# Side work beside the products of a hybrid attention and gating layer, laid out anew

## The chip, the cores and the metric

The kernel runs on one core of a Trainium2 chip. Its time is the device time of one execution in microseconds (us). Before the change the median of three runs is 1669.73 us (1668.16 to 1673.44). The engines are named as the profile names them: PE is TensorE (its weight loads are PEld), DVE is VectorE, ACT is ScalarE, POOL is GpSimd and SP is SyncE, which issues most of the DMAs; POOL issues the others.

## The reference, cut to what matters

One layer of a decoder trunk for 512 tokens of width 2048, in float32:

```python
shift, scale, gate = split(silu(c) @ w_ada + b_ada, 3)
h = rmsnorm(x, attn_norm_g) * (1 + scale) + shift
q_lat, kv_lat, k_rope, z_mla, u, v, z_sgu, g_mla, g_sgu = split(h @ w_in)
q  = rmsnorm(q_lat, q_norm_g) @ w_uq        # 16 heads, 128 + 64 rotary
kv = rmsnorm(kv_lat, kv_norm_g) @ w_ukv     # 16 heads, 128 + 128
y_mla = causal_attention(q, kv, rotary(k_rope)) * silu(z_mla)
y_sgu = u * (tril(w_spatial) @ rmsnorm(v) + b_spatial) * silu(z_sgu)   # 16 groups, chunks of 128
x = x + gate * ((sigmoid(g_mla) * y_mla + sigmoid(g_sgu) * y_sgu) @ w_out)
return rmsnorm(x, final_norm_g)
```

The widths are: q_lat 768, kv_lat 512, k_rope 64, and 2048 for each of z_mla, u, v, z_sgu, g_mla, g_sgu.

## The kernel before, in words

**Products.** Every float32 operand is split into a high part, which ACT makes by a cast, and a low part, which DVE makes by a subtraction (`hilo`, L139 to L141, and `split_to`, L92 to L112). Each product is then three matmuls, high by high, low by high and high by low (`mm3`, L134 to L137, and L1159 to L1161).

**The stages**, in order of the program:

1. The latents (q_lat, kv_lat) and one head's columns from x, weights w1 and w2. What the additive `shift` contributes to them (its "share") isn't in these products and is added much later.
2. v and k_rope, weights wv, in forty granules, each a weight tile with 24 matmuls. Beside it DVE makes the last third of the conditioning (`ada_dot`, 128x2048), scales the thirteen latent tiles by the norm of x and stores them in HBM (`lat_scale`), and forms sums and differences of blocks of h (`make_s12`, `make_s4`) for the next stage.
3. The pairs: the columns of z, g, u, s (z_sgu) and t (g_sgu) of two heads are taken as a pair, and their products with two halves of the tokens are done in seven products of half size instead of eight, after Strassen's scheme. There are 38 pairs. One of the seven products of a pair is a *step* (the code says slot) of 24 matmuls of 128x256. The steps are numbered -4 to 265; the steps -4 to -1 hold a plain product of one head's columns, and step 0 is the first of the pairs. Product p of pair k stands in a list `order`; products of one pair add up in one PSUM bank, and between two of them the bank's value is read out ("evacuated") by ACT (p = 1, 2, 4, 6) or DVE (p = 3, 5, 7).
4. Attention, 16 heads, then the output product and the last norm.

**What sets the order around the change.** The engines take their instructions strictly in the order in which the kernel's code issues them; there is no scheduler. In the pairs' stage an event is put on a step with `on(step, phase, f)`. Each step runs its events by phase: FIRST, EVAC, GATE, SPLIT, BACK ahead of the step's matmuls, MISC and LOAD behind them. The weight tile of step s is split in step s - 2 (SPLIT). Side work is put in BACK; loads and stores in LOAD. In the second stage the work of a granule hangs in `early[granule]`.

**The side work beside the pairs**, before the change:

- *Third differences* (`make_s3`, L742 to L746): for each of eight blocks of h, hh + hl, left half minus right half, split again; in BACK of steps -2 to 2. The results are the operands of product 3.
- *Spatial gating* (`sgu_*`): scale, split, 16 small matmuls, output, once for each of the 16 groups.
- *Share* (`share_load`, `share`, L840 to L860): w1 and w2 are loaded a second time, and DVE adds shift times each row block into four accumulators. One load of 512 KB (w1) or 320 KB (w2) into one buffer `raw3` every three steps, from step 44 on, and two DVE instructions three steps later; `shift_bias` sums them up from step 143 on.
- *Latents* (`lat_load`, `lat_sq`, `lat_rstd`, `lat_norm`, `last_gates`, L880 to L940): each latent tile (256 KB) comes back from HBM into one of two buffers (`rx`, `sinT`), first for the sum of squares, then, after the reciprocal root, to be normalised and stored again. A tile every two steps, loaded three steps ahead, steps 149 to 201.
- *Rotary tables* (`rope_part`, L946 to L1032): sine and cosine of position times frequency, in four quarters of 128 columns, two functions of a chain in each of 22 steps, 209 to 230. The last two functions of a quarter end in a Sin on ACT.
- *The rotary key*, steps 232 to 238, and the first splits for the attention at the end.

Of the kernel before, what the change touches and what calls it, by code (L numbers as in the profile page):

```python
# [20 lines left out]
P = 128  # L21
# [94 lines left out]
def trunk_layer(ctx, tc, xT, xn, c, vecs, pos, wada, w1, w2, wv, wv3, wv4, wh, wh15, wq, wqr, wk, wvv, wo, wsT, bsp, gfin, out,  # L116
# [340 lines left out]
    def split_sum(name, j, src):  # L457
        h, l = sums[name + "h"][:, j], sums[name + "l"][:, j]
        hilo(h, l, src)
# [10 lines left out]
    def make_s4(j):  # L470
        a, b = (nt(tb.p, [P, S], F32, f"t{i}") for i in range(2))
        tt(a[:, left], sums["s2h"][:, j].bitcast(F32), sums["s2l"][:, j].bitcast(F32), ALU.add)
        tt(b[:, left], hh[j + 8].bitcast(F32)[:, left], hl[j + 8].bitcast(F32)[:, left], ALU.add)
        tt(a[:, left], a[:, left], b[:, left], ALU.add)
        split_sum("s4", j, a[:, left])

    def lat_scale(i):
        tt(lat[i], lat[i], rx, ALU.mult)
        DMA.dma_start(lat_d[i], lat[i])

    for i in range(13):
        early.setdefault(8 + i, []).append(lambda i=i: lat_scale(i))
    for j in range(8):
        early.setdefault(11 + 2 * j + j // 2, []).append(lambda j=j: make_s12(j))
        early.setdefault(32 + j, []).append(lambda j=j: make_s4(j))
    for cg, w in enumerate(VW):
        psv = [bank()[:, :w] for _ in range(4)]
        for i in range(8):
# [17 lines left out]
            for f in early.pop(g, ()):  # L506
                f()
        if cg == 0:
# [6 lines left out]
        def evac_v(n, cg, ps):  # L515
            m = VW[cg] // P
            w, c0 = m * P, sum(VW[:cg])
            junk = nt(tb.p, [P, S], F32, "sig", bufs=2)
# [3 lines left out]
            DMA.dma_start(v_d[n][:, c0:c0 + w], t[:, :w])  # L522
            if cg == 4:
                DMA.dma_start(kr_d[n], t[:, w:VW[cg]])
# [313 lines left out]
    share_raw = [None]  # L838

    def share_load(k):  # L840
        share_raw[0] = t = nt(mis.p, [P, GW], F32, "raw3")
        if k < KC:
            DMA.dma_start(t, w1[k])
        else:
            DMA.dma_start(t[:, :640], w2[k - KC])

    def share(k):

        raw, j = share_raw[0], k % KC
        if k == 0:  # L850
            acc.extend([slot("rx"), slot("sinT")])
        if k == KC:
            acc.extend([slot("cosT"), acc2])
        for a, lo_, w in ((0, 0, S), (1, S, S)) if k < KC else ((2, 0, S), (3, S, P)):
            o, i_ = acc[a][:, :w], raw[:, lo_:lo_ + w]
            if j == 0:
                ts(o, i_, shift[:, 0:1], None, ALU.mult)
            else:
                stt(o, i_, shift[:, j:j + 1], o, ALU.mult, ALU.add)
# [21 lines left out]
    def lat_load(i, n):  # L881
        lat_in[i] = slot(("rx", "sinT")[n % 2])
        DMA.dma_start(lat_in[i], lat_d[i])

    def lat_sq(i):
        t = lat_in.pop(i)
        if i in (0, 6):
            ss[0] = slot("cosT")
# [6 lines left out]
    def lat_rstd(n):  # L895
        pl = bank()
        PE.matmul(pl, ones.bitcast(F32), ss[0], start=True, stop=True)
        rstd_from(ss[0], pl, n)

    def lat_norm(i):  # L900
        t = lat_in.pop(i)
        stt(t, t, bias[:, i:i + 1], ss[0], ALU.add, ALU.mult)
        on(done[0], LOAD, lambda: DMA.dma_start(latn_d[i], t))

    def last_gates(i):
# [9 lines left out]
        if i == 10:  # L915
            ss["g"] = slot("cosT")
# [4 lines left out]
        def to_u():  # L921
            DMA.dma_start(out_d["g"][1][7], ss["g"])
            ss["u"] = slot("cosT")
# [8 lines left out]
    s_, n = s_bias + 6, 0  # L932
    for f, a in todo:
        if f is lat_rstd:
            on(s_, MISC, f, a)
            s_ += 1
# [9 lines left out]
    def rope_part(half):  # L946
        w = S // 4
# [13 lines left out]
        def new(k):  # L961
            n = "cdes".find(k)
            t[k] = tables["ba".index(k)][:, cl] if n < 0 else rt[0][:, n * w:(n + 1) * w]
# [36 lines left out]
        def s9():  # L1000
# [3 lines left out]
            ACT.activation(tables[1][:, cl], t["d"], AF.Sin, scale=vec[:, C_SGN:C_SGN + 1])  # L1004

        def s10():
            ts(t["s"], t["s"], 0.25, None, ALU.add)
            rnd(new("e"), t["s"], m23)
            tt(new("d"), t["s"], t["e"], ALU.subtract)
            ts(t["d"], t["d"], lim, -lim, ALU.min, ALU.max)  # L1010
            ACT.activation(tables[0][:, cl], t["d"], AF.Sin, scale=2.0 * math.pi)

        rope.extend([s0, s1, s2, lambda: frac("c", c1_, True), lambda: frac("c", c2_),
                     lambda: frac("b", d1 / 65536.0), lambda: frac("b", d2 / 65536.0), s7, s8, s9, s10])

    for part in range(4):
# [3 lines left out]
    def rope_begin():  # L1020
        rt.append(slot("rx"))
        tables.extend([slot("cosT"), slot("sinT")])
        DMA.dma_start(tables[0].bitcast(I32), bcast(pos, S))

    s_ += 2
    on(s_, LOAD, rope_begin)
    for i in range(0, len(rope), 2):
        on(s_ + 4 + i // 2, BACK, lambda i=i: [f() for f in rope[i:i + 2]])
    s_ += 6 + len(rope) // 2
# [3 lines left out]
    def key_load():  # L1033
        krn = nt(mis.p, [P, GW], F32, "raw3")[:, :S].rearrange("p (n a b) -> p n a b", n=NB, a=2)
# [28 lines left out]
    on(s_, LOAD, key_load)  # L1063
    on(s_ + 4, MISC, key_turn)
# [489 lines left out]
```

## Time and profile before

| what | value |
|---|---|
| median of three runs | 1669.73 us |
| the profiled execution's own time | 1674.57 us |
| its span, first to last instruction | 1672.8 us |
| mean granted TensorE clock | 0.986 |
| PE busy | 1614.9 us (97%) |
| DVE, ACT, POOL busy | 1203.1 us (72%), 767.0 us (46%), 103.7 us (6%) |
| read from and written to HBM | 303.36 MB, 23.99 MB |

The first stage takes up to 195 us of the span, the second up to 342, the plain product and the pairs up to 1196, attention up to 1500 and the output product the rest. Times of rows are counted from the span's start. A busy PE isn't a PE at its peak: matmuls overlap, and half of a full clock looks as busy as the whole, so the profile's column of the granted clock (PEclk) has to be read with it. In the list of waits a row tells which instruction waited, for which, for how long in all, how often and how long at most. In a timeline a bracket at the end is the idle time of the engine just before that instruction, and what ended it.

### The profile page before, as it was taken

What the parts mean: (1) busy time and instruction counts of PE and PEld (TensorE: products, weight loads), DVE (VectorE), ACT (ScalarE), POOL (GpSimd) and SP (SyncE); (2) the same over time, 40 slices, a digit from 0 to 9 for tenths busy, and PEclk for the clock granted to TensorE, in tenths of its full rate; (3) what the DMA queues carried; (4) which work ended last, traced back from release to release, by engine and by line L of the source; (5) the groups of instructions that cost most, each with busy time, mean ns of one, the idle gap of its engine ahead of it and who ended that gap; (6) DMA issues with size and microseconds to landing.
All of it is one profiled execution on the core that took longest, in us unless ns stands there. A gap on an engine that the chain in (4) does not pass through costs nothing.

```text
span 1672.8 us, 27059 instructions
## 1 busy us (share of the span) xinstructions
PE 1614.9 (97%) x10760; PEld 1503.1 (90%) x10760; DVE 1203.1 (72%) x1840; ACT 767.0 (46%) x1272; POOL 103.7 (6%) x127
## 2 busy tenths in 40 slices
PE   9999999969999999999999898899999999999997
PEld 7888889969999999999999898799898888888887
DVE  8988677766667777777677678776778778874453
ACT  4343333445445444454554545454555555542332
POOL 0000000001111111111111011102000000000000
PEclk9999999989999999999999999999999999999999
DMA  9987588447789998988788886578523232326432
GB/s 378 347 294 289 194 288 296 149 129 201 209 206 253 250 254 223 254 246 228 203 223 232 236 239 177 122 194 170 177 85 102 85 101 80 98 76 252 126 101 101
DMA packets 116864, 329.13 MB, mean 197 GB/s; under 512 B 13545, under 2 KB 31489, under 8 KB 109953
## 3 DMA queue, kind: packets, MB, share of 16 engines
q1 hardware_dynamic: 99008, 269.72, 46.0%
q0 software_dynamic: 17728, 57.68, 19.9%
q8 instruction: 84, 1.38, 0.3%
q14 instruction: 44, 0.35, 0.1%
HBM read 303.36 MB, written 23.99 MB: 196 GB/s over the span
## 4 chain that ended last, share of the span: by engine, by line
PE 79%; DVE 9%; DMA 6%; ACT 3%; issue 2%; SPq 0%; DVEq 0%; ACTq 0%
PE ps L136 14%; PE ps L137 14%; PE ps L135 14%; PE ps L1159 11%; PE ps L1161 11%; PE ps L1160 11%; DMA rx<-lat_d 2%; DMA latn_d<-rx 1%; DVE lat L123 1%; DVE w2l L123 1%; PE ps L1321 1%; DVE w0l L123 1%; DVE rx L123 1%; DVE w1l L123 1%; PE ps L1284 1%
## 5 line engine op out<-in xcount | busy, mean ns | idle before, releaser
L1159 PE MATMUL ps<-hh,w2h 128*128 128x256 f32 x400 | 115.8, 289 | 8.1 <-DVE lat L123 5.6
L1159 PE MATMUL ps<-hh,w0h 128*128 128x256 f32 x416 | 118.9, 286 | 3.5 <-DVE lat L123 3.5
L1161 PE MATMUL ps<-hh,w0l 128*128 128x256 f32 x416 | 118.3, 284 | 1.0 <-DVE w0l L123 1.0
L1160 PE MATMUL ps<-hl,w0h 128*128 128x256 f32 x416 | 118.4, 285 | 0.0
L106 DVE TENSOR_TENSOR w1l<-wraw,w1h 128x1024 fp32r<-128x1024 f32 (+3 forms) x74 | 73.1, 988 | 62.4 <-ACT w1h L105 61.0
L106 DVE TENSOR_TENSOR w0l<-wraw,w0h 128x1024 fp32r<-128x1024 f32 (+3 forms) x74 | 78.9, 1066 | 53.2 <-ACT w0h L105 52.5
L1161 PE MATMUL ps<-hh,w2l 128*128 128x256 f32 x400 | 115.1, 288 | 1.8 <-DVE w2l L123 1.8
L1160 PE MATMUL ps<-hl,w2h 128*128 128x256 f32 x400 | 114.8, 287 | 0.0
L1159 PE MATMUL ps<-hh,w1h 128*128 128x256 f32 x400 | 113.9, 285 | 0.0
L1161 PE MATMUL ps<-hh,w1l 128*128 128x256 f32 x400 | 113.4, 284 | 0.1
L1160 PE MATMUL ps<-hl,w1h 128*128 128x256 f32 x400 | 113.3, 283 | 0.0
L105 ACT CAST w0h<-wraw 128x1024 fp32r<-128x1024 f32 (+3 forms) x74 | 68.9, 931 | 94.0 <-PE ps L137 47.1
L105 ACT CAST w1h<-wraw 128x1024 fp32r<-128x1024 f32 (+3 forms) x74 | 63.8, 862 | 99.3 <-PE ps L137 43.3
L126 DVE SCALAR_TENSOR_TENSOR wada<-wada,cact 128x2048 f32<-128x2048 f32 x47 | 107.1, 2281 | 0.0
L123 DVE TENSOR_TENSOR w2l<-raw,w2h 128x1024 fp32r<-128x1024 f32 x56 | 68.4, 1222 | 37.2 <-ACT w2h L616 37.1
L136 PE MATMUL ps<-w0l,hh 128*128 128x256 f32 (+3 forms) x288 | 93.3, 324 | 1.9 <-DVE w0l L106 1.9
L135 PE MATMUL ps<-w0h,hh 128*128 128x256 f32 (+3 forms) x288 | 93.6, 325 | 0.9 <-ACT w0h L105 0.9
L137 PE MATMUL ps<-w0h,hl 128*128 128x256 f32 (+3 forms) x288 | 93.1, 323 | 0.0
L137 PE MATMUL ps<-hh,w1l 128*128 128x512 f32 x226 | 88.9, 394 | 2.0 <-DVE w1l L106 2.0
L135 PE MATMUL ps<-hh,w1h 128*128 128x512 f32 x226 | 90.4, 400 | 0.2 <-ACT hh L378 0.2
L136 PE MATMUL ps<-hl,w1h 128*128 128x512 f32 x226 | 88.9, 393 | 0.8 <-DVE hl L126 0.8
L596 POOL DMA_DIRECT2D wraw<-in_wh x66 | 58.5, 941 | 462.1 <-DVE w0l L123 203.6
(351 smaller groups left out, 5475.6 us busy)
## 6 DMA issues: line engine op xcount, KB each, us to landing
raw<-in_wh SPq DMA_DIRECT2D x105, 512.0 KB, 7.1
wada<-in_wada SPq DMA_DIRECT2D x47, 1024.0 KB, 7.2
wraw<-in_wh POOLq DMA_DIRECT2D x66, 512.0 KB, 7.1
wraw<-in_wh SPq DMA_DIRECT2D x45, 512.0 KB, 7.6
raw<-in_wh POOLq DMA_DIRECT2D x42, 512.0 KB, 7.1
wraw<-in_wo SPq DMA_DIRECT2D x32, 512.0 KB, 3.7
wraw<-in_w SPq DMA_DIRECT2D x16, 512.0 KB, 8.5
wraw<-in_wv SPq DMA_DIRECT2D x16, 512.0 KB, 4.8
```

What stands on the lines that cost most here:

```text
L105: self.nc.scalar.copy(hi[:, :n], raw[:, :n])
L106: self.nc.vector.tensor_tensor(out=lo[:, :n], in0=raw[:, :n], in1=hi[:, :n].bitcast(F32), op=ALU.subtract)
L123: DVE.tensor_tensor(out=out, in0=in0, in1=in1, op=op)
L126: DVE.scalar_tensor_tensor(out=out, in0=in0, scalar=scalar, in1=in1, op0=op0, op1=op1, **kw)
L135: PE.matmul(ps, ah, bh, start=start, stop=False)
L136: PE.matmul(ps, ah, bl, start=False, stop=False)
L137: PE.matmul(ps, al, bh, start=False, stop=stop)
L596: q_.dma_start(t, wh[h, n, q // 10 - 1], **eng)
L1159: PE.matmul(ps, wH[:, sl], xh, start=st, stop=False, skip_group_check=True)
L1160: PE.matmul(ps, wH[:, sl], xl, start=False, stop=False, skip_group_check=True)
L1161: PE.matmul(ps, wL[:, sl], xh, start=False, stop=sp, skip_group_check=True)
L1284: PE.matmul(ps, q2[:, q], krh[:, :n], start=False, stop=False)
```

## The change

Eight edits, none of which adds or removes a matmul:

1. **Third differences.** `make_s12`, `make_s4` and `make_s3` become one `make_sums` in the second stage. DVE forms all four results there; the first two are split one granule later, the third (kept in float32 in freed latent tiles) only in BACK of steps -2 to 1, two a step, and the fourth in granules 32 to 39.
2. **Stores of the second stage.** Stores of v, k_rope and the latents are put in a list and issued a granule later. The latents are scaled in another order, so that tiles come free in the order in which the sums need them. The squares in `evac_v` no longer share the two buffers of the stored copies.
3. **Share.** 52 loads of 256 KB in place of 32 of 512 or 320 KB, two buffers `half0` and `half1`, one load every two steps, four steps ahead, one DVE instruction of 512 columns each (the last four: four of 128 columns).
4. **Latents.** They use `half0` and `half1`; loads stand four steps ahead; a normalised tile comes every three steps and not every two, and is stored in MISC of the next step. `ss` moves from `cosT` to `rx`.
5. **Reciprocal.** The 128x512 reciprocal is cut into four of 128x128, one in each of four steps.
6. **Rotary tables.** Two halves of 256 columns instead of four quarters, one function a step, in steps 166 to 177 and 201 to 212 instead of 209 to 230; both Sin stand in a function of their own at the end of each half. The latents now run over steps 154 to 221, the share over 42 to 149.
7. **Rotary key.** Its steps are unchanged (232 to 238).
8. **First splits of the attention.** One step earlier.

```diff
-    def make_s12(j):
-        a, b = (nt(tb.p, [P, S], F32, f"t{i}") for i in range(2))
+    def make_sums(j):
+        a, b = (nt(tb.p, [P, S], F32, f"t{i}") for i in range(2))
         tt(a, hh[j].bitcast(F32), hl[j].bitcast(F32), ALU.add)
-        tt(b[:, right], hh[j + 8].bitcast(F32)[:, right], hl[j + 8].bitcast(F32)[:, right], ALU.add)
+        tt(b, hh[j + 8].bitcast(F32), hl[j + 8].bitcast(F32), ALU.add)
+        s3f[j], s4f[j] = half_of(S3_AT, j), half_of(S4_AT, j)
+        tt(s3f[j], a[:, left], a[:, right], ALU.subtract)
         tt(b[:, right], a[:, right], b[:, right], ALU.subtract)
-        split_sum("s1", j, b[:, right])
-        tt(b[:, left], b[:, right], a[:, left], ALU.subtract)
-        split_sum("s2", j, b[:, left])
...
+        tt(a[:, left], b[:, right], a[:, left], ALU.subtract)
+        tt(s4f[j], a[:, left], b[:, left], ALU.add)
+        return lambda: (split_sum("s1", j, b[:, right]), split_sum("s2", j, a[:, left]))
...
+    def stores():
+        for dst, src in leaving:
+            DMA.dma_start(dst, src)
+        leaving[:], made[:] = made[:], []
...
-    def make_s3(j):
-        a = slot(("rx", "lat12")[j % 2])
-        tt(a, hh[j].bitcast(F32), hl[j].bitcast(F32), ALU.add)
-        tt(a[:, left], a[:, left], a[:, right], ALU.subtract)
-        hilo(hh[j][:, right], hl[j][:, right], a[:, left])
-
     for j in range(8):
-        on(-2 + j * 2 // 3, BACK, make_s3, j)
+        on(-2 + j // 2, BACK, lambda j=j: hilo(hh[j][:, right], hl[j][:, right], s3f[j]))
...
-    s_share = base[6] + 4
-    for k in range(2 * KC):
-        on(s_share + 3 * k, LOAD, share_load, k)
-        on(s_share + 3 * k + 3, BACK, share, k)
-    s_bias = s_share + 6 * KC + 3
+    s_share = base[6] + 2
+    for i in range(len(shares)):
+        on(s_share + 2 * i, LOAD, share_load, i)
+        on(s_share + 2 * i + 4, BACK, share, i)
+    s_bias = s_share + 2 * len(shares) + 4
...
     def lat_rstd(n):
...
-        rstd_from(ss[0], pl, n)
+        ACT.activation(ss[0], pl, AF.Sqrt, bias=eps, scale=1.0 / n)
+        r = ss[0]
+        for q in range(4):
+            on(done[0] + 1 + q, BACK, lambda o=r[:, q * P:(q + 1) * P]: DVE.reciprocal(out=o, in_=o))
...
     def lat_norm(i):
         t = lat_in.pop(i)
         stt(t, t, bias[:, i:i + 1], ss[0], ALU.add, ALU.mult)
-        on(done[0], LOAD, lambda: DMA.dma_start(latn_d[i], t))
+        on(done[0] + 1, MISC, lambda: DMA.dma_start(latn_d[i], t))
...
-            on(s_ - 3, LOAD, lat_load, a, n)
+            on(s_ - 4, LOAD, lat_load, a, n)
...
-        s_ += 2
+        s_ += 3 if f is lat_norm else 2
...
+    on(base[22] + 9, LOAD, rope_begin)
+    for part in range(2):
+        s_ = base[22 + 5 * part] + 14
+        on(s_, FIRST, rope_places)
+        for i in range(12):
+            on(s_ + i, BACK, rope[12 * part + i])
...
-    on(n_slots - 1, SPLIT, lambda: ws.split_to(gr[0]))
+    on(n_slots - 2, SPLIT, lambda: ws.split_to(gr[0]))
+    on(n_slots - 1, MISC, lambda: ws.split_to(gq[0]))
```

**DVE at the opening of the pairs.** Before, its rows between the weight splits of steps 2 and 3 (`w1l`, `w0l`) hold two whole third differences: a sum of 512 columns, a difference of 256 and the low part, twice.

```order
L123 TENSOR_TENSOR lat_334_3159<-hh_158_1272,hl_160_1276 128x512
L123 TENSOR_TENSOR lat_334_3159<-lat_334_3159 128x256
L123 TENSOR_TENSOR hl_160_1276<-lat_334_3159,hh_158_1272 128x256
L123 TENSOR_TENSOR rx_3164<-hh_165_1352,hl_167_1356 128x512
L123 TENSOR_TENSOR rx_3164<-rx_3164 128x256
L123 TENSOR_TENSOR hl_167_1356<-rx_3164,hh_165_1352 128x256
L123 TENSOR_TENSOR lat_338_3197<-lat_330_3151,lat_331_3153 128x512
L123 TENSOR_TENSOR w0l_3200<-raw_311_3033,w0h_3199 128x1024
```

Now the rows there are the low parts alone (`lat_260` is a kept third difference), and the next step's rows follow.

```order
L123 TENSOR_TENSOR hl_167_1356<-lat_260_2373,hh_165_1352 128x256
L123 TENSOR_TENSOR hl_168_1358<-lat_260_2373,hh_166_1354 128x256
L123 TENSOR_TENSOR lat_325_3168<-lat_319_3128,lat_320_3130 128x512
L123 TENSOR_TENSOR w0l_3171<-raw_303_3017,w0h_3170 128x1024
L123 TENSOR_TENSOR hl_175_1416<-lat_282_2583,hh_173_1412 128x256
L123 TENSOR_TENSOR hl_176_1418<-lat_282_2583,hh_174_1414 128x256
L123 TENSOR_TENSOR raw_300_3011<-raw_300_3011,raw_302_3015 128x1024
```

The sums and differences have gone to the second stage; ACT's casts of the high parts stay where they were, two a step.

**SP in the latents' norms.** Before, the store of a normalised tile (`latn_d`) stands right behind the load of the tile after next, and a load into its buffer one weight load later.

```order
L883 DMA rx_9448<-lat_d_110 128x512
L903 DMA latn_d_122<-sinT_9380 128x512
L596 DMA raw_1128_9511<-in_wh 128x1024
L883 DMA sinT_9513<-lat_d_111 128x512
L903 DMA latn_d_123<-rx_9448 128x512
```

Now the store (`latn_d_120` from buffer `half_1129`) stands in the following step, and the next load into the same buffer (`half_1154`) behind one weight load; the loads for the spatial gating (`wsr`, `bsr`, `lat` from `v_d`) stand behind that load.

```order
L928 DMA latn_d_120<-half_1129_9507 128x512
L616 DMA raw_1153_9714<-in_wh 128x1024
L905 DMA half_1154_9716<-lat_d_109 128x512
L771 DMA wsr_9748<-in_wsT 128x256
L773 DMA bsr_9750<-in_bsp 128x256
L778 DMA lat_1159_9752<-v_d 128x4x128
L928 DMA latn_d_121<-half_1141_9612 128x512
```

What moved is the distance: a tile of the norms comes every third step, with the same order of store and load in the queue.

**DVE in the rotary tables.** Before, a step's rows are two functions of a quarter (128 columns), here with the gates' rows and the weight split `w1l` of the step after.

```order
L130 TENSOR_SCALAR rx_10530<-cosT_10531 128x128
L132 TENSOR_SCALAR rx_10530<-rx_10530 128x128
L123 TENSOR_TENSOR rx_10530<-rx_10530 128x128 x2
L132 TENSOR_SCALAR rx_10530<-rx_10530 128x128
L123 TENSOR_TENSOR rx_10530<-rx_10530 128x128
L126 SCALAR_TENSOR_TENSOR sinT_10532<-rx_10530,sinT_10532 128x128
L123 TENSOR_TENSOR lat_1238_10330<-lat_1238_10330,lat_1283_10744 128x512
L123 TENSOR_TENSOR lat_1238_10330<-lat_1251_10439,lat_1238_10330 128x512
L123 TENSOR_TENSOR w1l_10787<-wraw_1268_10596,w1h_10786 128x1024
```

Now they are one function of a half (256 columns), and every other step a latent's sum of squares stands ahead of it (`rx`, last row but four).

```order
L130 TENSOR_SCALAR lat_1083_9100<-cosT_8939 128x256
L132 TENSOR_SCALAR lat_1084_9101<-lat_1083_9100 128x256
L123 TENSOR_TENSOR lat_1083_9100<-lat_1083_9100,lat_1084_9101 128x256
L123 TENSOR_TENSOR lat_1084_9101<-lat_1084_9101,lat_1083_9100 128x256
L123 TENSOR_TENSOR lat_1091_9143<-ps_1109_9297,lat_1091_9143 128x256
L123 TENSOR_TENSOR wraw_1082_9096<-wraw_1082_9096,wraw_1089_9139 128x1024
L123 TENSOR_TENSOR w0l_9326<-wraw_1082_9096,w0h_9325 128x1024
L123 TENSOR_TENSOR rx_8952<-rx_8952,lat_1112_9329 128x512
L130 TENSOR_SCALAR lat_1083_9100<-cosT_8939 128x256
L132 TENSOR_SCALAR lat_1084_9101<-lat_1083_9100 128x256
L123 TENSOR_TENSOR lat_1083_9100<-lat_1083_9100,lat_1084_9101 128x256
L123 TENSOR_TENSOR lat_1084_9101<-lat_1084_9101,lat_1083_9100 128x256
```

The tables have moved from steps that hold no other side work but the gating to steps that hold the latents' work too.

More of the change, by code (lines that the diff above doesn't have):

```diff
@@ L477, in lat_scale, with store @@
+        tt(s4f[j], a[:, left], b[:, left], ALU.add)
+        return lambda: (split_sum("s1", j, b[:, right]), split_sum("s2", j, a[:, left]))
+    made, leaving = [], []
+    def store(dst, src):
+        made.append((dst, src))
+    def stores():
+        for dst, src in leaving:
+            DMA.dma_start(dst, src)
+        leaving[:], made[:] = made[:], []
     def lat_scale(i):
         tt(lat[i], lat[i], rx, ALU.mult)
-        DMA.dma_start(lat_d[i], lat[i])
-    for i in range(13):
-        early.setdefault(8 + i, []).append(lambda i=i: lat_scale(i))
+        store(lat_d[i], lat[i])
@@ L837, in trunk_layer, with half_raw, share_load, share @@
     acc = []
[L838 to L843, printed above, removed]
-        else:
[L845 to L856, printed above, removed]
+    share_raw = {}
+    def half_raw(i):
+        return nt(mis.p, [P, S], F32, f"half{i % 2}")
+    shares = [(q, (k,), w1[k][:, q * S:(q + 1) * S]) for k in range(KC) for q in range(2)]
+    shares += [(2, (k,), w2[k][:, :S]) for k in range(KC)]
+    shares += [(3, range(k, k + 4), w2[k:k + 4][:, :, S:640]) for k in range(0, KC, 4)]
+    def share_load(i):
+        q, ks, src = shares[i]
+        share_raw[i] = t = half_raw(i)
+        if q == 3:
+            DMA.dma_start(t.rearrange("p (k w) -> p k w", w=P), src.rearrange("k p w -> p k w"))
+        else:
+            DMA.dma_start(t, src)
+    def share(i):
+        q, ks, _ = shares[i]
+        raw, w = share_raw.pop(i), S // len(ks)
+        if len(acc) <= q:
+            acc.append(slot(("rx", "sinT", "cosT")[q]) if q < 3 else acc2)
+        for n, k in enumerate(ks):
+            o, i_ = acc[q][:, :w], raw[:, n * w:(n + 1) * w]
+            if k == 0:
                 ts(o, i_, shift[:, 0:1], None, ALU.mult)
             else:
-                stt(o, i_, shift[:, j:j + 1], o, ALU.mult, ALU.add)
+                stt(o, i_, shift[:, k:k + 1], o, ALU.mult, ALU.add)
     def shift_bias(m0):
```

80 lines of the change are left out of this document (43 added, 37 removed).

## The prediction

> **What bounds the kernel now.** First the page's head, for the share of each engine.
>
> ```profile
> span 1672.8 us, 27059 instructions
> PE 1614.9 (97%) x10760; PEld 1503.1 (90%) x10760; DVE 1203.1 (72%) x1840; ACT 767.0 (46%) x1272; POOL 103.7 (6%) x127
> ```
>
> PE is busy for 97% of the span, and the change leaves every matmul in place, so all that can be won is time in which PE stands or runs at half clock. To see where that is I cut the span into windows at the stages that the change touches (busy time and instructions of each engine, then the granted clock, the DMA share and GB/s).
>
> ```profile
> core 0: us, PE busy (x) PEld busy (x) DVE busy (x) ACT busy (x) POOL busy (x), PEclk, DMA share, GB/s
> 200.00:340.00 140.00, 137.64 (x751) 129.10 (x750) 104.34 (x153) 51.28 (x102) 0.00 (x0) 0.99 0.74 250
> 340.00:361.00 21.00, 19.16 (x110) 16.67 (x108) 12.01 (x21) 9.34 (x22) 0.98 (x1) 1.00 0.46 130
> 361.00:372.00 11.00, 0.08 (x2) 0.05 (x1) 7.32 (x12) 4.63 (x9) 0.00 (x0) 0.64 0.00 0
> 372.00:378.00 6.00, 6.00 (x29) 6.00 (x30) 4.38 (x7) 1.45 (x2) 0.86 (x1) 0.53 0.59 188
> 530.00:610.00 80.00, 77.73 (x646) 77.29 (x645) 60.63 (x75) 37.42 (x55) 10.28 (x12) 1.00 0.90 248
> 610.00:830.00 220.00, 220.00 (x1835) 219.77 (x1835) 165.40 (x218) 107.78 (x164) 27.43 (x32) 1.00 0.88 235
> 830.00:855.00 25.00, 21.99 (x169) 21.58 (x168) 14.79 (x20) 11.05 (x19) 2.58 (x3) 0.93 0.84 228
> 855.00:1015.00 160.00, 153.73 (x1241) 151.70 (x1240) 114.47 (x146) 81.82 (x117) 17.99 (x21) 0.98 0.85 230
> 1015.00:1100.00 85.00, 69.34 (x517) 66.75 (x516) 69.06 (x172) 46.35 (x69) 7.78 (x9) 0.94 0.59 147
> 1176.00:1216.00 40.00, 36.32 (x242) 33.10 (x241) 28.06 (x38) 22.48 (x35) 0.00 (x0) 0.96 0.55 183
> ```
>
> The row 610 to 830 is the pairs undisturbed: 220 us for 1835 matmuls, 0.120 us each, so a step of 24 takes 2.88 us. Where a window of the pairs holds fewer, what is lost is its length less 0.120 times its count; this takes in gaps and half clock together. So:
>
> - 530 to 610 loses 80 − 646 × 0.120 = 2.5 us;
> - 830 to 855 loses 25 − 169 × 0.120 = 4.7;
> - 855 to 1015 loses 160 − 1241 × 0.120 = 11.1;
> - 1015 to 1100 loses 85 − 517 × 0.120 = 23.0.
>
> The others hold matmuls of other shapes, so I take idle time and clock apart. 200 to 340: 2.36 idle and 1% of 140 = 1.4 for the clock, 3.8. The opening of the pairs, 340 to 378: 1.84 and 10.92 idle, and 6 − 29 × 0.120 = 2.5 at a clock of 0.53, 15.3. 1176 to 1216: 3.68 idle and 4% of 40 = 1.6, 5.3. Together 65.7 us can be won here at most.
>
> Then the waits, PE's own and the one of ACT that matters (waiter, for whom; us in total, times, longest).
>
> ```profile
> PE ps L1159 <- ACT lat L717: 13.7, 3, 10.9
> PE ps L1159 <- DVE lat L123: 9.2, 5, 3.4
> ```
>
> ```profile
> ACT s1h L140 <- DVE t L123: 29.6, 8, 4.8
> ```
>
> The longest stall of PE, 10.9 us, waits for an evacuation on ACT. The timeline of the opening, DVE and then ACT, tells what ACT stood behind.
>
> ```profile
> 364.12 0.68 DVE L123 TENSOR_TENSOR lat<-hh,hl 128x512 f32<-128x512 f32 x1
> 364.84 0.42 DVE L123 TENSOR_TENSOR lat<-lat 128x256 f32<-128x256 f32 x1
> 365.73 0.42 DVE L123 TENSOR_TENSOR hl<-lat,hh 128x256 fp32r<-128x256 f32 x1 [0.47 <-ACT hh L140]
> ```
>
> ```profile
> 371.22 0.40 ACT L140 CAST hh<-lat 128x256 fp32r<-128x256 f32 x1 [2.35 <-DVE lat L123]
> 371.53 0.37 ACT L717 COPY lat<-ps 128x256 f32<-128x256 f32 x1
> ```
>
> A third difference is three DVE rows, and ACT's cast waits in order for the second of them; the evacuation of 0.37 us at 371.53, which PE wants, stands behind the last such cast. So the stall is DVE's work, reaching PE through ACT's queue.
>
> **The change part by part.** Durations of DVE's operations, by group with shapes kept apart (busy, mean ns of one, idle before and its cause):
>
> ```profile
> L123 DVE TENSOR_TENSOR w2l<-raw,w2h 128x1024 fp32r<-128x1024 f32 x56 | 68.4, 1222 | 37.2 <-ACT w2h L616 37.1
> L123 DVE TENSOR_TENSOR lat<-lat,lat 128x512 f32<-128x512 f32 x92 | 62.9, 685 | 0.6
> ...
> L123 DVE TENSOR_TENSOR t<-t,t 128x256 f32<-128x256 f32 x24 | 10.1, 423 | 0.5
> ```
>
> (b) *Opening.* In steps -1 to 3, five steps of 2.88 = 14.4 us, DVE's order before holds 7 rows of 128x1024, 9 of 128x512 and 16 of 128x256: 7 × 1.22 + 9 × 0.68 + 16 × 0.42 = 21.4 us, 7.0 too many. After it holds 7, 1 and 8: 12.6, which is 1.8 less than there is time for. The eight sums and eight differences, 8 × (0.68 + 0.42) = 8.8 us, are gone; the eight casts and low parts stay, and no cast waits any more for a difference. What is late next is the evacuation itself: product 7 follows product 6 in one bank, and ACT still makes casts and the first sigmoid there. I leave 2.5 of the 15.3; between 1.2 (almost nothing left) and 7 (ACT late by itself). Gain **12.8**, 8 to 14.
>
> (a) *Second stage.* For each of eight blocks the four sums took one row of 512 columns and six of 256; now they take two and four: 8 × (0.685 − 2 × 0.423) = −1.3 us for DVE, though the differences are added. The splits stand a granule behind the sums, so the 29.6 us of ACT's waiting for `t` should go, and with it the late casts of weights. What is late next is DVE itself: a granule with sums holds 2 × 0.685 + 4 × 0.423 = 3.1 us of them in one piece, beside the conditioning's and weight rows. I leave 1.3 of 3.8: gain **2.5**, −2 to 3.8. The stores go a granule later past the loads on SP's queue; they only read.
>
> (c) *Share.* In the same groups the first accumulator's row ends in a wait for the load:
>
> ```profile
> L126 DVE SCALAR_TENSOR_TENSOR rx<-raw,shift,rx 128x512 f32<-128x512 f32 x15 | 11.2, 748 | 12.3 <-DMA raw<-in_w 12.3
> ```
>
> A load stands three steps ahead, 8.6 us, but behind its buffer's last reader. Two buffers and four steps, 11.5 us, take that wait. DVE's work stays: the same 64 rows, 48 of 512 columns and 16 of 128. Gain **2.2** of 2.5, 0 to 2.5. The landing times that this rests on, by DMA group (KB each, median us to landing):
>
> ```profile
> raw<-in_w SPq DMA_DIRECT2D x16, 512.0 KB, 6.3
> ...
> rx<-lat_d SPq DMA_DIRECT2D x12, 256.0 KB, 6.6
> ```
>
> Half the size lands no sooner here, 6.6 against 6.3 us, so 52 loads might ask more of the DMA engines than 32. The Trainium skill's page "DMA: Bandwidth & Descriptors", section "Bandwidth", speaks against such a cut: it would have transfers batched to a MiB or more, since each carries a fixed cost, in "Anatomy of one DMA" about 2.0 us. By that page an estimate of 20 × 2.0 = 40 us is added, against 300 us × 0.12 = 36 us free; the sum would be some 4 us smaller. The row of 6.6 us doesn't part fixed cost from a queue's length; its price is a rival below.
>
> (d) *830 to 855.* The last gates pass an accumulator through HBM:
>
> ```profile
> 836.19 0.75 DVE L126 SCALAR_TENSOR_TENSOR cosT<-rx,bias,cosT 128x512 f32<-128x512 f32 x1 [4.22 <-DMA cosT<-t_d]
> ```
>
> ```profile
> 847.02 0.39 PE L1159 MATMUL ps<-s1h,w2h 128*128 128x256 f32 x1 [2.26 <-ACT w2h L616]
> ```
>
> In the changed code the same load and wait stand there, in `rx`. Gain **0**, −3 to 3.
>
> (e) *Latents, 855 to 1015.* The norms wait for their loads as well:
>
> ```profile
> L126 DVE SCALAR_TENSOR_TENSOR rx<-rx,bias,cosT 128x512 f32<-128x512 f32 x5 | 3.7, 748 | 8.6 <-DMA rx<-lat_d 8.6
> ```
>
> By the list of DMA groups a tile's store lands after 7.3 us:
>
> ```profile
> latn_d<-rx SPq DMA_DIRECT2D x5, 256.0 KB, 7.3
> ```
>
> A load follows the store of the tile before in the same buffer, 7.3 + 6.6 = 13.9 us of landings, with three steps (8.6 us) ahead. Now a tile comes every three steps: the store a step later, the load a step behind that, four steps ahead of its use. From the norm to the next norm in the same buffer six steps pass, 17.3 us, and store and load, 13.9, begin about one step in, 2.9: 16.8, so it just fits. The reciprocal of 512 columns goes into four pieces, which the trace has elsewhere:
>
> ```profile
> L227 DVE RECIPROCAL cosT<-cosT 128x512 f32<-128x512 f32 x2 | 6.7, 3350 | 2.3 <-ACT cosT L226 2.3
> ```
>
> ```profile
> L445 DVE RECIPROCAL rx<-rx 128x128 f32<-128x128 f32 x4 | 3.8, 947 | 1.2 <-ACT rx L436 1.2
> ```
>
> One of 3.35 us is longer than a step, one of 0.947 isn't. I leave 2.0 (0.5 us of slack won't do at each of ten tiles): gain **9.1** of 11.1, 4 to 11.
>
> (f) *Rotary tables.* The rows of the old tables, and the nearest for a scalar operation of 256 columns:
>
> ```profile
> L123 DVE TENSOR_TENSOR rx<-rx 128x128 f32<-128x128 f32 x40 | 11.7, 292 | 1.5
> ```
>
> ```profile
> L132 DVE TENSOR_SCALAR rx<-rx 128x128 f32<-128x128 f32 x36 | 8.3, 231 | 1.1
> ```
>
> ```profile
> L130 DVE TENSOR_SCALAR hl<-hl,mx 128x256 f32<-128x256 f32 x16 | 5.7, 353 | 0.6
> ```
>
> Before, steps 213 to 231 hold, by rows of the order, 22 × 1.22 + 9 × 0.685 + 10 × 0.42 + 4 × 0.48 and 108 rows of 128 columns (0.26 in the mean of the two kinds), 67 us, against 19 × 2.88 = 54.7: 12 too many, of which came a loss of 23.0, about double, since ACT's casts and the half clock add to it.
> The tables take 34 DVE rows a part. Four parts of 128 columns, at 0.26: 35 us; two of 256, at 0.39: 26.5. So 9 us are gone outright. But the halves now meet the latents. Steps 171 to 179 hold 11 × 1.22 + 6 × 0.685 + 16 × 0.423 + 12 × 0.353 + 4 × 0.947 = 32.3 us, against 25.9: 6.4 over. Steps 206 to 213 hold 9 × 1.22 + 4 × 0.685 + 15 × 0.423 + 12 × 0.353 + 0.75 + 4 × 0.947 = 28.8, against 23.0: 5.8 over. Weights are split two steps ahead, so DVE may be late by about a step less an evacuation, 2.88 − 0.42 = 2.5, before PE waits (an estimate). What is left is 3.9 + 3.3 = 7.2 us. With before's doubling it would be 14.4. I take 8: it comes in bits under 0.7 us a step, far below the gap of 2.26 us (row in (d)) in whose window the clock fell to 0.93. Gain 23.0 − 8 = **15.0**; ends 5 (18 left, neither slack nor cover) and 17. What is left stands at two places, about 865 and 965 us.
>
> (g) *Start of attention.* The wait here is for a weight's low part:
>
> ```profile
> 1198.89 0.50 PE L137 MATMUL ps<-hh,w1l 128*128 128x512 f32 x1 [1.96 <-DVE w1l L106]
> ```
>
> The split now stands a step earlier, and a second one in the last step. Left are the waits that rest on loads: gain **3.3** of 5.3, 1 to 4.
>
> Sum: 12.8 + 2.5 + 2.2 + 0 + 9.1 + 15.0 + 3.3 = 44.9 us. The profiled execution took 1674.57 (span 1672.8); it would take 1629.7. It lies 4.84 above the median of the runs, 1669.73, which becomes **1625** (1624.8). The rows' unfavourable ends, taken together as independent (roots of squares: 4.8, 4.5, 2.2, 3, 5.1, 10, 2.3), are 14 below the sum; the favourable ones all at once 10 above. The forecast's own range is 1615 to 1639.
>
> **The rivals.**
>
> *A, the rotary steps are overfull again.* If ACT's casts and sigmoids stand behind DVE there, as they did at 1015 to 1100, the 12.2 us over cost double, 24, and nothing is won in (f); and the norms beside them keep 7 of their 11.1. For it: the two humps of the order, and the doubling before. Against it: 9 us less work. 2.5 + 12.8 + 2.2 + 4 + 3.3 = 24.8: **1645**.
>
> *B, all of it is hidden.* Only (d) stays: 65.7 − 4.7 = 61: **1609**. For it: DVE busy for 165 of 220 us in the undisturbed stretch, where PE never waits. Against: the humps.
>
> *C, slower: SP is held in the norms.* A store waits on SP for DVE's norm, and the load into the same buffer for that store's landing, 7.3 us. What SP has behind it is weight loads:
>
> ```profile
> raw<-in_wh SPq DMA_DIRECT2D x105, 512.0 KB, 7.1
> ```
>
> They are issued about six steps, 17.3 us, ahead, so once SP has fallen behind by 10 us, PE waits. If a load holds SP until the store ahead of it has landed, and the next norm and its store wait for that load, a tile takes 7.3 + 6.6 = 13.9 us, not its three steps of 8.6: 5.3 us for each of ten tiles, 53, and up to 2.5 of half clock behind each (the opening's), so 53 to 78; with 65, and without (e)'s 9.1, the sum is 44.9 − 9.1 − 65 = −29: **1699**. For it: the queue is in order, and the gating's loads stand behind too. Against: before had the same pair in the queue at two steps a tile, and lost 11.1 there in all.
>
> *D, nothing moves.* The second stage or the latents get what the opening gives up: about **1669**. Against: DVE's work there falls by 1.3 us.
>
> *E, the cut share loads fill the DMA engines.* If 256 KB ask as much as 512, 52 loads are 26.6 MB in place of 16 × 0.51 + 16 × 0.32 = 13.3: 13.3 MB at 235 GB/s is 57 us, where 36 are free in 300 us: 21 lost, **1646**. Against: the equal landings may only be the queue's length.
>
> **How the numbers follow.** Forecast 0.60, A 0.12, B 0.10, C 0.07, D 0.06, E 0.05. About 0.3%, 5 us, is what a measurement of this kernel can tell from no change. Faster: forecast, A, B, E, 0.87; same: D, 0.06; slower: C, 0.07. The range 1608 to 1650 takes in the forecast's, A, B and E; it leaves out C and D, 0.13, and what misses by the unknown ends, some 0.07.
>
> **What would show it.** Right: 361 to 372 busy on PE throughout; no cast of `s1h` that waits for `t`; no wait for `raw<-in_w`; 1015 to 1100 at 0.120 us a matmul; what is left of losses at 865 and 965, as gaps under 2.26 us at full clock. Wrong: DVE waits for `lat_d` of over a us at each norm (C), a half clock between 860 and 990 (A), a DMA share near 1.00 from 500 to 800 with waits on weights (E), or a gap above 5 us that is left at the opening, which would say that ACT's own work, not DVE's differences, sets it.

## The result, and the profile after

The median is 1628.84 us (four runs, 1626.13 to 1630.45) beside 1669.95 for the kernel before (four runs too: the three known ahead of the prediction and one more); the ratio is 0.975, with an interval of 0.9729 to 0.977. The profiled execution took 1629.12 us. Its page begins:

```profile
span 1627.4 us, 26972 instructions
...
PE 1600.6 (98%) x10760; PEld 1492.2 (92%) x10760; DVE 1181.3 (73%) x1754; ACT 757.0 (47%) x1262; POOL 103.8 (6%) x127
```

The windows, cut where the stages now lie (columns as before):

```profile
200.00:326.00 126.00, 125.91 (x684) 117.64 (x683) 99.29 (x143) 46.71 (x95) 0.00 (x0) 1.00 0.75 253
326.00:358.00 32.00, 31.25 (x200) 29.15 (x200) 15.92 (x25) 17.31 (x38) 0.98 (x1) 1.00 0.59 175
515.00:590.00 75.00, 75.00 (x628) 75.00 (x627) 55.78 (x68) 34.74 (x50) 8.56 (x10) 1.00 0.91 246
815.00:858.00 43.00, 40.61 (x335) 39.99 (x334) 31.22 (x46) 22.12 (x34) 4.46 (x6) 1.00 0.83 221
858.00:885.00 27.00, 25.52 (x205) 24.66 (x205) 24.95 (x45) 17.52 (x23) 3.33 (x4) 1.00 0.76 210
...
915.00:940.00 25.00, 22.95 (x190) 22.58 (x190) 17.81 (x23) 11.81 (x20) 2.56 (x3) 1.00 0.92 265
...
965.00:1000.00 35.00, 32.50 (x250) 31.44 (x249) 31.14 (x53) 19.71 (x25) 4.27 (x6) 0.95 0.71 199
1000.00:1130.00 130.00, 129.93 (x1085) 129.76 (x1084) 88.07 (x105) 65.11 (x97) 21.69 (x23) 1.00 0.81 201
1155.00:1172.00 17.00, 12.02 (x63) 10.59 (x62) 8.39 (x12) 6.56 (x9) 0.00 (x0) 0.80 0.53 172
```

The second stage, the opening, the share and everything behind 1000 us run without a loss worth the name; what is left by the count of matmuls is 43 − 335 × 0.120 = 2.8 us at 815 to 858, 2.4 at 858 to 885, 2.2 at 915 to 940 and 5.0 at 965 to 1000. New is the last row: at the start of the attention PE stands for 5 of 17 us at a clock of 0.80. PE's two largest waits say the same:

```profile
PE ps L1194 <- DVE lat L123: 6.0, 4, 2.1
PE ps L135 <- ACT w0h L105: 4.3, 1, 4.3
```

Both programs issue 10,760 matmuls in the same order, but for a few small ones of the side work that stand elsewhere, so the start of each can be set against its start before. From one stage to the next this lead grows by:

| term of the sum | predicted gain, us | measured |
|---|---|---|
| (a) second stage | 2.5 | 4.05 |
| (b) opening | 12.8 | 15.0 |
| (c) share | 2.2 | 3.2 |
| (d), (e), (f) together, 815 to 1130 | 24.1 | 25.4 |
| (g) start of attention | 3.3 | −3.0 |
| sum, with 0.5 ahead of the first change | 44.9 | 45.2 |

(The sum of the rows and the 0.5 is 45.2.) Within (d), (e), (f), what the windows leave is 2.8 for (d), 2.2 for the norms at 920 and 2.4 + 0.2 + 5.0 = 7.6 for the tables, 1.3 of it a stretch of half clock at 988 (last section); the prediction left 4.7, 2.0 and 8.

### The profile page after: what moved, and what is told of

Same layout as the page of the kernel before. It is cut to its first block, busy times and chain, and to the rows that moved or that the text cites. A ratio compares the mean times of both kernels' runs of the same rounds, so it can differ in the third digit from the quotient of the medians.

```text
span 1627.4 us, 26972 instructions
## 1 busy us (share of the span) xinstructions
PE 1600.6 (98%) x10760; PEld 1492.2 (92%) x10760; DVE 1181.3 (73%) x1754; ACT 757.0 (47%) x1262; POOL 103.8 (6%) x127
## 4 chain that ended last, share of the span: by engine, by line
PE 82%; DVE 8%; DMA 5%; ACT 2%; issue 2%; SPq 1%; DVEq 0%; ACTq 0%
PE ps L136 14%; PE ps L137 14%; PE ps L135 14%; PE ps L1194 12%; PE ps L1196 12%; PE ps L1195 12%; DVE lat L123 1%; DMA half<-lat_d 1%; PE ps L1356 1%; DMA latn_d<-half 1%; DVE w0l L123 1%; DVE wada L126 1%; PE ps L1319 1%; DVE w2l L123 1%; PE ps L1320 1%
```

## The experiments

A gain "at a place" is worked out as in the table, from the starts of the same matmuls, against the kernel named. That is needed because places that an edit doesn't touch differ by 1 to 3 us from profile to profile, mostly by a stretch of half clock that comes or doesn't (last section).

### end_undone and end_load: the start of the attention

```diff
-    on(n_slots - 2, SPLIT, lambda: ws.split_to(gr[0]))
-    on(n_slots - 1, MISC, lambda: ws.split_to(gq[0]))
+    on(n_slots - 1, SPLIT, lambda: ws.split_to(gr[0]))
```

> The changed kernel with edit 8 undone (one split, in the last step). Theory 1, from the changed trace: with the earlier splits PE comes to the first v product sooner than the load of its weights, which stands in SP's queue behind the stores of the last pair; that costs a gap of 4.30 us and 6.8 us of half clock, and the stage loses 8.4 us where it lost 5.3 before. Undone, the three waits on DVE's low parts (0.85, 1.96, 0.87 us) come back, the gap of 4.30 goes, and the kernel is 3 us faster than the changed one: a span of 1624.4. Theory 2, the prediction's: the earlier splits are worth 3.3 us and the 4.30 came from something else: 3.3 us slower, a span of 1630.7.

Median 1626.31, ratio 0.9739 (0.9722 to 0.9756). At the place it is 3.5 us faster than the changed kernel; the span is 1625.5, since 1.5 went elsewhere. So edit 8 costs time here.

```diff
     on(n_slots - 1, MISC, lambda: ws.split_to(gq[0]))
+    on(n_slots - 1, LOAD, first_weights, 3)
```

> The changed kernel with the load of the first v weights issued in the last step, ahead of the last pair's stores in SP's queue (its buffer is free since the split of two steps before). Theory 1: the gap of 4.30 us and the half clock behind it go, 8.4 us of loss become about 1: a span of 1620. Theory 2: the load is late because its buffer or the memory is, not for its place in the queue: a gap of 3 to 4 us stays and the span is within 1.5 us of 1627.4.

Median 1622.99, ratio 0.9725 (0.971 to 0.9739), 7.3 us faster at the place, span 1622.4. SP's timeline of the changed kernel, then ACT's row:

```profile
1153.45 0.93 SPq L723 DMA_DIRECT2D t_d<-lat  x2
...
1156.44 0.38 SPq L86 DMA_DIRECT2D wraw<-in_wvv  x1
```

```profile
1162.77 1.04 ACT L105 CAST w0h<-wraw 128x1024 fp32r<-128x1024 f32 x1 [5.30 <-DMA wraw<-in_wvv]
```

and both for end_load:

```profile
1150.64 0.33 SPq L86 DMA_DIRECT2D wraw<-in_wvv  x1
...
1155.76 0.93 SPq L723 DMA_DIRECT2D t_d<-lat  x2
```

```profile
1159.67 1.06 ACT L105 CAST w0h<-wraw 128x1024 fp32r<-128x1024 f32 x1
```

The load of the first v weights stood behind two stores that wait for the last gates' value; issued 5 us ahead of them it has no bracket: nobody waits for it. Theory 1 holds in both at the place, to within half a us; the spans lie 1.1 and 2.4 us above what it gave, because other places lost 1.5 and 2.3.

### u_in_sinT: the row of the last gates

```diff
-            ss["u"] = slot("rx")
+            ss["u"] = slot("sinT")
```

> The changed kernel with the u gate's tile read back into sinT and not into rx. Theory 1: at 834.70 ACT waits 5.49 us for a store out of rx before it may write the first square there, and DVE and PE behind it (6.36, and 0.66, 0.98 and 0.76 us); with the tile elsewhere nothing waits for that store, and 2.4 to 2.9 us of the span go: 1624.5 to 1625. Theory 2: the wait only passes to the next transfer of the row of gates, and less than 0.7 us are won.

Median 1624.22, ratio 0.9733 (0.9719 to 0.9747). At the place 3.2 us are won, a little more than theory 1 gave, and the three waits of PE there are gone; the span is 1622.3, since another 1.9 was won elsewhere. The row of the changed kernel that it removes, ACT's:

```profile
834.70 0.72 ACT L911 ACTIVATE rx<-half,bias 128x512 f32<-128x512 f32 x1 [5.49 <-DMA t_d<-rx]
```

ACT waited for a store to have read `rx`, and every cast behind it waited too.

### rope_spread: the two humps

```diff
-        on(s_, FIRST, rope_places)
+        on(s_ - 1, FIRST, rope_places)
         for i in range(12):
-            on(s_ + i, BACK, rope[12 * part + i])
+            on(s_ + 7 * i // 4, BACK, rope[12 * part + i])
```

> The changed kernel with the twelve functions of each half of the rotary tables spread over 20 steps (offsets 7i/4) and not over 12 in a row; the work is the same. Theory 1: the loss of some 8 us at 858 to 890 and 965 to 1000 is DVE's backlog, up to 4.8 us by the rows of the order; spread, it stays under 3.1, and 5 to 6.5 us go: a span of 1621 to 1622.5. Theory 2: what is lost there comes from ACT's table loads (a Sin, a square root and a sigmoid in turn) or from the latents' loads, which all stay: within 1.5 us of 1627.4.

Median 1626.53, ratio 0.9747 (0.9733 to 0.9762), span 1624.3: between the two theories. Its windows, with the wait of DVE at 919 us:

```profile
865.00:890.00 25.00, 24.67 (x200) 23.98 (x200) 23.27 (x38) 14.03 (x20) 3.97 (x5) 1.00 0.66 169
...
915.00:927.00 12.00, 8.71 (x61) 8.53 (x60) 6.02 (x10) 4.21 (x6) 0.84 (x1) 0.86 0.82 275
975.00:992.00 17.00, 16.72 (x140) 16.55 (x139) 16.66 (x28) 8.57 (x12) 2.56 (x3) 1.00 0.81 204
```

```profile
919.24 0.75 DVE L126 SCALAR_TENSOR_TENSOR half<-half,bias,rx 128x512 f32<-128x512 f32 x1 [3.07 <-DMA half<-lat_d]
```

The humps gave 2.0 and 4.2 us, the 6.2 that theory 1 asks for. Up to 2.1 of that may be chance: end_undone, which leaves the tables alone, won 0.6 in the first, and end_load 1.5 in the second, where the half clock at 988 stayed out. 2.9 went back at 920, where PE now came earlier to a norm whose load came no earlier (a gap of 3.29 us for 1.90, and half clock behind it). What is left, 4.1 or more, speaks for DVE's backlog: in the changed kernel PE's gaps of 1.21 us at 877.66 and 2.06 at 987.38 both end with a row of DVE, which stood idle for 0.28 us in the 11 us ahead of the first and not at all in the 11 ahead of the second. The run doesn't part this wholly from theory 2, because the Sin moved as well: each, with a table load of 1.28 us on either side, went from 879 and 989 us to 901 and 1010. The loads did not all stay, as theory 2 had it, but none was saved.

### norm2 and norm4: the spacing of the norms

```diff
-        s_ += 3 if f is lat_norm else 2
+        s_ += 2
```

(norm2; its loads stand three steps ahead and its stores in LOAD of their own step, as in the kernel before. norm4 has the 3 made a 4 and nothing else.)

> The changed kernel with the latents' spacing of before: a normalised tile every two steps, stored in LOAD of its own step, loads three steps ahead. Theory 1: the chain of norm, store, load and norm in one buffer takes some 17 us and has four steps (11.5 us) again; the norms wait some 12 us in all for lat_d, as before, and PE loses 4 to 8 us more between 890 and 1000: a span of 1631 to 1635. Theory 2: the gain in that window came from the cut reciprocal and the tables that moved, not from the spacing: within 2 us of 1627.4.

Median 1634.76, ratio 0.9787 (0.9774 to 0.9801), span 1630.6, just under what theory 1 gave. DVE's list of waits has the load again, in the changed kernel and then here:

```profile
DVE half L126 <- DMA half<-lat_d: 2.4, 1, 2.4
```

```profile
DVE half L126 <- DMA half<-lat_d: 9.6, 4, 3.4
```

From 897 to 973 us 4.4 us are lost against the changed kernel; 1.4 comes back later, where its half clock at 988 is missing. Theory 1 had the mechanism, but put 4 to 8 us between 890 and 1000, of which 3.0 are left, and 12 us on the waits, which are 9.6.

> The changed kernel with a normalised tile every four steps and not every three. Theory 1: what is lost at 920 us (DVE 2.44 us for half from lat_d, PE 1.90 us) is the chain of norm, store, load and norm in one buffer, some 17 us that just fits into six steps (17.3 us); with eight (23 us) no norm waits for its load, and 2 to 2.5 us go; the second reciprocal moves by six steps off the middle of the second half of the tables, which takes 1 to 2 more: a span of 1623 to 1625. Theory 2: the load is late because the memory is busy (265 GB/s and a share of 0.92 there): the wait stays, and the span is within 1.5 us of 1627.4.

Median 1624.02, ratio 0.9734 (0.972 to 0.9749), span 1621.5. The norms' wait falls from 2.4 to 0.7 us; 2.1 us are won at 920, 2.6 in the second half of the tables (0.5 of it from the half clock there) and 1.3 of the 5.9 at the start of attention, where the gap and the half clock were shorter. The chain can be read off SP in the changed kernel:

```profile
892.99 0.33 SPq L928 DMA_DIRECT2D latn_d<-half  x1
894.46 0.33 SPq L616 DMA_DIRECT2D raw<-in_wh  x1
902.01 0.33 SPq L905 DMA_DIRECT2D half<-lat_d  x1
```

The load stands in SP's queue from 894.8 on and is issued at 902.01, when the store out of its buffer has landed, 9 us after its issue. Ahead of this load and the two that follow it SP is held for 7.2, 5.8 and 7.3 us, which is the mechanism of the slower rival (C); at three steps a tile it cost one norm, not ten, and no matmul between 885 and 940 us waited over 0.2 us for a weight.

### sums_only and splits_now: the third differences

sums_only is the kernel before with the diff's first part and `stores` alone.

> The kernel before with edits 1 and 2 alone (the third differences and the stores of the second stage). Theory 1, the prediction's: the opening of the pairs and the second stage gain by themselves what the changed kernel gains there, 15.0 and 4.1 us, and nothing later moves: a span of 1672.8 - 19.1 = 1653.7, the rest of the losses as before. Theory 2: part of it is given back later (the lead shrinks between 380 and 1200 us) or needs the other edits: a span over 1657.

Median 1651.68, ratio 0.9907 (0.9887 to 0.9926). Against before it wins 3.8 us in the second stage and 15.1 in the opening, as the changed kernel does. The span is 1648.3, under what was expected, by 5.7 us at places that it doesn't touch: 1.6 at the share and 2.3 at 850 us among them. wide_old and wide_sin below, which have the old code there too, won 2.1 and 2.0 at the share and 3.2 and 2.9 at 850. So of (c) and (d) up to that much is not the edits' doing. The opening of sums_only:

```profile
320.00:354.00 34.00, 33.86 (x214) 31.76 (x212) 15.03 (x25) 19.04 (x43) 0.99 (x1) 1.00 0.67 190
354.00:378.00 24.00, 23.41 (x195) 23.42 (x196) 16.34 (x20) 12.13 (x21) 2.58 (x3) 1.00 0.77 214
```

splits_now is the changed kernel with the casts in the sums' own granule:

```diff
-        early.setdefault(at_ + 1, []).insert(0, make_sums(j))
+        make_sums(j)()
```

> The changed kernel with the splits of the first two sums in the same granule as the sums, not one later. Theory 1: ACT's casts then stand in order behind DVE's sums again, with some 30 us of waiting for t, weights are cast late, and the 4.05 us that the changed kernel won at 258 to 305 are lost: a span of 1631.4. Theory 2: the gain there came from less work on DVE and the tiles that come free in order: within 1 us of 1627.4.

Median 1630.11, ratio 0.9771 (0.9755 to 0.9787), span 1629.3. The second stage loses 4.5 us, all of term (a); 2.6 come back at places that the edit doesn't touch, hence the span. ACT's waits there, in the changed kernel and then here:

```profile
ACT s1h L140 <- DVE t L123: 3.8, 6, 1.1
```

```profile
ACT s1h L140 <- DVE t L123: 32.5, 8, 6.0
```

The work on DVE is the same in both: it is the granule between sum and cast that pays.

### wide_old and wide_sin: the tables in their old steps

```diff
-        w = S // 4
+        w = S // 2
...
-    for i in range(0, len(rope), 2):
-        on(s_ + 4 + i // 2, BACK, lambda i=i: [f() for f in rope[i:i + 2]])
+    for i in range(len(rope)):
+        on(s_ + 4 + i, BACK, rope[i])
```

> The kernel before with the rotary tables made in two halves of 256 columns, one function a step, in the old steps 209 to 230 (the work tiles in raw3, which is free there); nothing else is changed. Theory 1: the loss of 23.0 us at 1015 to 1100 is DVE's excess of 12 us with what ACT and the clock add; the halves take 9 us of work away, the excess falls to 3, little more than what passes unnoticed, and 18 to 23 us go: a span of 1650 to 1655. Theory 2: the place counts, not the width (beside the gating's rows and with Sin on ACT): 8 to 12 us go, a span of 1661 to 1665.

Median 1657.63, ratio 0.9938 (0.9921 to 0.9955), span 1655.5. At the place 10.7 us are won of the 23.0, half of what theory 1 asked for. The halves have not only fewer DVE rows but also four Sin and four table loads (1.28 us each) fewer on ACT, so the 10.7 are for both. The number is theory 2's; its reason was left to the next kernel. ACT's waits in the window 1010 to 1085:

```profile
ACT sinT L1004 <- DVE raw L132: 5.4, 2, 3.1
...
ACT cosT L1011 <- DVE raw L132: 3.9, 2, 2.6
```

wide_sin takes both Sin out of the chain's last functions and puts them into one of their own, a step later.

> The kernel wide_old (halves of 256 columns in the old steps) with both Sin of a half in a function of their own, one step behind the last of DVE's. Theory 1: what wide_old still lost at 1015 to 1085, some 12 us, comes in part from ACT, which stood 9.3 us in its four Sin, waiting in order for DVE's last row while casts and evacuations stood behind; with Sin a step later that waiting goes, and 4 to 8 us more are won: a span of 1648 to 1652, of which the part up to 1000 us is as in wide_old. Theory 2: Sin only shows where DVE is late; DVE's backlog is what PE waits for, and less than 2 us are won over wide_old (1655.5).

Median 1650.8, ratio 0.9886 (0.9872 to 0.9899), span 1646.7. At the place 19.6 us of 23.0 are won, 8.9 more than in wide_old, where theory 1 gave 4 to 8. ACT's waits ahead of the Sin, 9.3 us in wide_old, are gone; two table loads more are saved as well, 2.6 us of ACT, since the two Sin of a half now follow each other, and no run parts the two. The window 1010 to 1085 in wide_old, then in wide_sin:

```profile
1010.00:1085.00 75.00, 66.66 (x522) 64.49 (x521) 59.68 (x110) 41.23 (x62) 7.81 (x10) 0.98 0.67 167
```

```profile
1010.00:1085.00 75.00, 72.75 (x597) 71.62 (x596) 65.66 (x120) 42.27 (x64) 8.76 (x11) 1.00 0.74 185
```

DVE is busier in the second and PE loses 3.4 us in place of 12.4. Where the tables stand was not what cost; their width and the Sin were. The new steps, among the latents, are where the 7.6 us of humps came from.

### best: four edits on the changed kernel

`end_load`, `u_in_sinT`, `rope_spread` and `norm4` together.

> The changed kernel with four edits together: the load of the first v weights in the last step, the u gate's tile in sinT, the tables' functions spread over 20 steps, a normalised tile every four steps. Theory 1: each took its own loss (7.3, 3.2, 6.2 in the two humps, 2.1 at 920), and the wait for lat_d that rope_spread met at 920 isn't there with four steps: 17 to 19 us together, a span of 1608.5 to 1610.5. Theory 2: what one of them wins is given back at the next wait, as rope_spread's first hump was at 920: under 13 us, a span over 1614.

Median 1610.63, ratio to before 0.9648 (0.9635 to 0.9661), span 1608.0: 19.4 us under the changed kernel, a little over theory 1; 1.0 of it was won ahead of 190 us, which no edit touches. Its page:

```profile
span 1608.0 us, 26972 instructions
...
PE 1595.3 (99%) x10760; PEld 1488.6 (93%) x10760; DVE 1181.3 (73%) x1754; ACT 758.0 (47%) x1262; POOL 104.2 (6%) x127
```

No wait of PE is over 1.1 us in it.

## Why the prediction was right, and where it wasn't

- **The sum.** 44.9 us were forecast, the profiled execution shows 1674.57 − 1629.12 = 45.5, and 1629.7 was forecast for it. That the two agree so closely is luck in part: (g) fell short by 6.3 us, and the other rows, with the 0.5 ahead of them, came out 6.6 above theirs. The median was to be 1625 and is 1628.84, 41.1 us under before's: the prediction carried over the 4.84 us by which before's profiled execution lay above its median, and the new one lies only 0.3 above.
- **(b) and (a)** were right in mechanism (sums_only, splits_now) and too low: 15.0 for 12.8 and 4.05 for 2.5. The step that was mis-sized is "what is late next": an evacuation on ACT that keeps 2.5 us, and DVE's lumps in the granules that keep 1.3. They kept 0.75 (32.00 − 31.25 in the row from 326 us) and 0.09 (126.00 − 125.91).
- **(c)** came as forecast in its number, 3.2 for 2.2, but only in part by its mechanism. With the old loads in place sums_only won 1.6 us there, wide_old 2.1 and wide_sin 2.0, although in sums_only DVE still waited 9.3 us for them with the rows of `rx`. So the runs leave 1.1 to 1.6 us to the edit; the rest came without it. Rival E didn't come: the DMA share at 515 to 590 is 0.91 after 0.90 before, with PE busy for all 75 us, so 52 loads of 256 KB did not ask as much as 52 of 512; nor did the 4 us show that the prediction worked out from a fixed cost of each load.
- **(d)** was to be 0; 1.9 us were won, but sums_only, with the old code there, won 2.3. The wait itself is real and stayed: u_in_sinT took 3.2 us.
- **(e)** right in size: one norm of ten still waits, and 2.2 us are left for 2.0. norm2 and norm4 show the chain of store and load as the cause of that wait, and of 4.4 of the 8.9 us won. The cut reciprocal was not run by itself. Before, the stretch of the first reciprocal lost next to nothing, that of the second 35 − 270 × 0.120 = 2.6 us:

```profile
855.00:885.00 30.00, 30.00 (x248) 29.52 (x247) 22.58 (x27) 17.85 (x25) 2.56 (x3) 1.00 0.89 259
940.00:975.00 35.00, 33.12 (x270) 32.23 (x269) 24.81 (x30) 22.84 (x37) 2.57 (x3) 1.00 0.79 206
```

- **(f)** right in size, 7.6 us left for 8, at the two places named (865 and 965), and rope_spread, which only spreads the rows, took 6.2 of them, 4.1 at the least beyond chance. They did not come as bits under 0.7 us at full clock, as forecast, but with gaps of 1.21 and 2.06 us and half clock behind the second. One step failed: that the old loss of 23.0 was DVE's excess, doubled by what hung on it, so that 9 us less work would take most of it. The halves, with four Sin fewer, took 10.7 (wide_old); 8.9 more came with the Sin in a function of its own (wide_sin minus wide_old), which the prediction didn't price. That rival A's doubling didn't come in the new steps fits this: there the Sin stands apart.
- **(g)** wrong in sign. The step was "Left are the waits that rest on loads: gain 3.3 of 5.3, 1 to 4". The splits did take PE's waits at 1198 away, and the lead grew by 3.9 us, but the load that was next in line stands behind the last pair's stores on SP; PE came to it earlier, stood for 4.30 and 0.68 us, and lost some 3.4 more to a clock of 0.80 over 17 us, where before lost 1.5 at that place: −6.9, so −3.0 in all. SP's queue was in the trace of before, where the load was issued 3 us behind `t_d`, at 1200.80:

```profile
1203.78 0.38 SPq L86 DMA_DIRECT2D wraw<-in_wvv  x1
```

```profile
1209.90 1.05 ACT L105 CAST w0h<-wraw 128x1024 fp32r<-128x1024 f32 x1 [0.74 <-DVE lat L123]
```

The load landed 6.0 us after its issue, at 1209.8, and its cast began 0.1 us later; in the changed kernel issue and cast lie 6.3 us apart. That load had no slack to give, and this could have been read.

## What to carry to other kernels

Where an engine takes its work strictly in order, put a step between the instruction that makes a value and the one on another engine that reads it: the granule ahead of the casts was worth 4.5 us at no change in work, the step ahead of the Sin, with two table loads saved, 8.9. When a wait is taken away, look up the next load that the freed engine comes to, and what stands ahead of it in its queue. A buffer that is normalised in place and stored turns over only as fast as norm, store and load land one after another.

## What the runs showed of the hardware

The same gap may or may not have half a clock behind it. PE waited 2.06 us at the same matmul in the changed kernel and in end_load:

```profile
987.38 0.36 PE L1194 MATMUL ps<-hh,w1h 128*128 128x256 f32 x1 [2.06 <-DVE lat L123]
```

```profile
991.17 0.35 PE L1195 MATMUL ps<-hh,w1h 128*128 128x256 f32 x1 [2.06 <-DVE lat L123]
```

Behind it, the 3.4 us windows of the two:

```profile
988.60:992.00 3.40, 3.40 (x18) 3.40 (x17) 3.33 (x6) 2.48 (x5) 0.85 (x1) 0.51 0.46 159
```

```profile
991.20:994.60 3.40, 3.40 (x29) 3.40 (x29) 3.30 (x7) 3.37 (x5) 0.00 (x0) 1.00 0.37 107
```

18 matmuls against 29, some 1.3 us. So a gap of about 2 us has a price that varies from run to run, and a difference of 1 to 3 us at a place that an edit doesn't touch is no finding. The Trainium skill's page "TensorE: Matmul & The Clock Gate", section "Part 1: The HAM clock gate", says that the gate watches a free-running window and that its effect varies between runs; these rows agree with the second, and no run here shows the window itself. It also gives about 3.4 us of idling as what throttles; here half a clock followed a gap of 2.06 us, and the rows decide.
